# Inverting the diagonal blocks of all RWKV heads in one 128-partition loop instead of two 64-partition loops

## The chip, the cores and the metric

One core of a Trainium2 chip runs the whole program. The metric is the device time of one execution in microseconds, taken as the median of several runs. The engines are TensorE (PE for its matrix products, PEld for loading the stationary operand), VectorE (DVE), ScalarE (ACT), GpSimd (POOL) and SyncE (SP, which here issues nearly all DMAs). Each engine works through its own queue strictly in order and waits on semaphores for the others.

## What is computed

Two layers of a hybrid block (a pooling mixer, a retention branch, an RWKV-7 branch, three gated merges), followed by one attention layer and a mixture of experts. There are 512 tokens of width 1024. The change touches the RWKV-7 branch of each of the two layers. Its recurrence per head is, in the reference:

```
def step(S, inp):
    r_t, w_t, k_t, v_t, a_t, b_t = inp
    sa = jnp.einsum('bhvk,bhk->bhv', S, a_t)
    S = (S * w_t[:, :, None, :] + sa[..., None] * b_t[:, :, None, :]
         + v_t[..., None] * k_t[:, :, None, :])
    return S, jnp.einsum('bhvk,bhk->bhv', S, r_t)
```

There are 8 heads of width 64. The kernel does not walk the 512 tokens one by one: it cuts them into 8 chunks of 64 and solves, for each head and chunk, a unit triangular system of size 64. For this it inverts the two diagonal blocks of 32 x 32 of each system by elimination and puts the inverse of the whole together with two small products.

## The kernel before

The 8 heads are worked in two halves of 4 heads (`hf` 0 and 1). For one half there are three pieces of work, each a Python generator:

- `rwkv_prep` (line 557) scales the operands with the decay (DVE, ACT, POOL and a few products on PE), computes the masked products of all chunks (lines 635 to 651, called Gram products below; they go to DRAM as `gd`), and then inverts the diagonal blocks. For this, `lt` gets the blocks from DRAM with one block on each partition: 32 systems (4 heads by 8 chunks) times 2 diagonal blocks, so 64 partitions (line 667). The elimination has 31 turns of two DVE instructions each, a product into `tmp` (line 674) and an addition into `tt` (line 676); turn j works on (j+1)(31-j) elements of each partition, between 31 and 256. Then ACT turns one block over (line 681), and three DMAs write the results back to DRAM (lines 682 and 684), where the recurrence reads them.
- `rwkv_chain` (line 688) is the recurrence over the 8 chunks: a chain of small products on PE, with copies on DVE and ACT between them. Its products are tied one to the next by hand, and the first product of the next dense tile is tied behind them (`self.pin`), so PE can't run past a product of the recurrence that waits.
- `rwkv_out` (line 842) normalises and adds.

These generators run as side work of the dense matmuls, which fill PE with three passes (high and low parts) over each weight tile. `mm3` (line 309) calls `tick`, and each `tick` advances the side work: a dense tile with 8 contraction blocks gives two steps of it, one with 4 blocks gives one. A `yield` ends a step. What is emitted in which step decides the program order; a planner then orders each engine's queue by its own estimate of when an instruction is ready, and program order ranks the ready ones.

In `rwkv` (line 503) the first half's prep comes first (19 steps). Then the recurrence of half 0, which idles `CHAIN_WAIT` = 24 steps before its first loads, goes in turn with the prep of half 1, which waits `PREP_WAIT` = 6 steps and until its projections exist. The recurrence of half 1 follows with the output of half 0. `layer` (line 1095) starts this side work right after the projections of half 0; the retention branch (`rows_of` at 952, the projections of half 1, then q and k tiles with `rotary` at 1017), the pooling branch and the two first merges run meanwhile, and `self.drain(rs)` (line 1122) runs what is left of it before the third merge.

The dense weights pass through `split` (line 298): ACT rounds the high part, DVE (every fifth time POOL) subtracts it to get the low part `wlo` (line 306). PE needs both before it can run the tile, so DVE and ACT feed PE at every tile.

Of the kernel before, what the change touches and what calls it, by code (L numbers as in the profile page):

```python
# [11 lines left out]
F32 = mybir.dt.float32  # L12
F32R = mybir.dt.float32r
I32 = mybir.dt.int32
AF = mybir.ActivationFunctionType
OP = mybir.AluOpType
# [8 lines left out]
NC_ = T // C  # L25
# [150 lines left out]
class Layers:  # L176
# [324 lines left out]
        return out  # L501

    def rwkv(self, l, t, wa, out):
        prep = lambda hf: self.rwkv_prep(l, hf, t[hf][0:2], t[hf][2:4], t[hf][4:6], wa)
        ops = yield from prep(0)
        ys, nxt = yield from self.both(self.rwkv_chain(l, *ops, wait=CHAIN_WAIT), self.late(t, prep))
        (_, ys) = yield from self.both(self.rwkv_out(0, ys, ops[3]), self.rwkv_chain(l, *nxt))
        yield from self.rwkv_out(1, ys, nxt[3])
        out += ops[3] + nxt[3]

    def late(self, t, prep):
        for _ in range(PREP_WAIT):
            yield
        while len(t) < 2:
            yield
        return (yield from prep(1))

    def both(self, *gens):

# [37 lines left out]
    def rwkv_prep(self, l, hf, r, k, v, wa):  # L557

        nc, c = self.nc, self.c
# [4 lines left out]
        for i in range(2):  # L564
            p = 2 * hf + i
# [10 lines left out]
        DC = self.S("DC", [128, 2, NC_], "DC", 2)  # L576
        AR, BK, bv = [], [], []
        for i in range(2):
            p = 2 * hf + i
# [48 lines left out]
            nc.vector.tensor_mul(bk[:, :, :C], b3(kk), b3(di))  # L628
            AR.append(ar)
            BK.append(bk)  # L630
            yield

        nu = 4 * NC_
        gd = self.dr.tile([128, nu, 128], F32, name=f"gd{l}{hf}")
        for ch in range(0, NC_, 2):
            g = [self.RM() for _ in range(2)]
            m = None
            for j in range(4):
                for h2 in range(2):
                    r2 = slice(64 * h2, 64 * h2 + 64)  # L640
                    m = self.mm(g[h2][:, j * 128:j * 128 + 128], BK[j % 2][r2, ch + j // 2, :],
                                AR[j % 2][r2, ch + j // 2, :], start=True, stop=True, after=m)
            for h2 in range(2):
# [11 lines left out]
        if hf == 0:  # L655
            ad = self.dr.tile([128, 2, NC_, 128], F32, name=f"ad{l}")
            for i in range(2):
                nc.sync.dma_start(ad[:, i], AR[i])
            AR = ad

        lt = self.S("lt", [2 * nu, 32, 32], "b", NB)
        tt = self.S("tt", [2 * nu, 32, 32], "b", NB)
        nc.gpsimd.memset(tt, 0.0)
        nc.gpsimd.memset(tt.rearrange("p a b -> p (a b)")[:, ::33], 1.0)
        blk = lambda f: gd[32 * f:32 * f + 32, :, 32 * f:32 * f + 32].rearrange("s u t -> u s t")
        for f in range(2):
            nc.sync.dma_start(lt[nu * f:nu * f + nu], blk(f))
        yield
        yield
        tmp = self.S("tmp", [2 * nu, 16 * 16], "tmp", 1)  # L670
        for j in range(31):
            n = 31 - j
            t = tmp[:, :(j + 1) * n].rearrange("p (s t) -> p s t", s=j + 1)
            nc.vector.tensor_tensor(t, tt[:, 0:j + 1, j:j + 1].to_broadcast([2 * nu, j + 1, n]),  # L674
                                    lt[:, j:j + 1, j + 1:].to_broadcast([2 * nu, j + 1, n]), op=OP.mult)
            nc.vector.tensor_add(tt[:, 0:j + 1, j + 1:], tt[:, 0:j + 1, j + 1:], t)  # L676
            if j % 8 == 7:
                yield
        tn = self.dr.tile([32, nu, 32], F32, name=f"tn{l}{hf}")
        tu = lt[0:nu]  # L680
        nc.scalar.activation(tu, tt[0:nu].rearrange("p s t -> p t s"), AF.Copy)
        nc.sync.dma_start(tn.rearrange("t u s -> u t s"), tu)
        for f in range(2):
            nc.sync.dma_start(blk(f), tt[nu * f:nu * f + nu])
        yield
        return AR, BK, v, bv, DC, gd, tn

    def rwkv_chain(self, l, AR, BT, v, bv, DC, gd, tn, wait=0):

        nc, c = self.nc, self.c  # L690
        ident = c["ident"]
        u_of = lambda hd: (hd % 2) * 2 + hd // 2
        gts, ars, tis, xxs, brs, uvs, qys, ys = {}, {}, {}, {}, {}, {}, {}, []
# [62 lines left out]
            nc.vector.tensor_copy(q, qys[ch][0:64, :256])  # L756
            return q

        for _ in range(wait):
            yield  # L760
        for ch in range(3):
            load(ch)
        load_ar(1)
# [12 lines left out]
        for ch in range(NC_):  # L776
# [15 lines left out]
            if not last:  # L792
                for i in range(2):
                    for h2 in range(2):
                        s = slice(64 * h2, 64 * h2 + 64)
# [11 lines left out]
            if not last:  # L807
                for h2 in range(2):
                    s = slice(64 * h2, 64 * h2 + 64)
# [9 lines left out]
            o = 256 * (ch % 4 // 2)  # L819
# [1113 lines left out]
NB = 8  # L1933
# [5 lines left out]
ATT_RATE = 4.0  # L1939
NEX = 5  # L1940
NOH = 3
CHAIN_WAIT = 24
PREP_WAIT = 6


# [14 lines left out]
```

## Time and profile before

| | |
|---|---|
| median of 3 runs | 1994.51 us (1987.49 to 1998.53) |
| the profiled execution | 1992.5 us, its span from first to last instruction 1990.4 us |
| granted TensorE clock, mean | 0.959 of full speed |
| busy share of the span | PE 93%, DVE 55%, ACT 30%, POOL 26% |

The profile is of one execution. "Busy" of an engine is the time in which one of its instructions ran. The granted clock is given as a share of full speed: 1.0 is 2.4 GHz, 0.5 is 1.2 GHz, and a value between is a mean over a stretch with both. A matmul at half clock is busy for longer and does no more, so a stretch loses time for PE in two ways: it stands idle, or it runs at the low clock.

### The profile page before, as it was taken

How to read it: one execution, taken by the hardware profiler on the slowest of the kernel's cores; microseconds unless marked ns; L12 is line 12 of the kernel's file. 1: busy time of each engine (PE TensorE's matmuls, PEld its weight loads, DVE VectorE, ACT ScalarE, POOL GpSimd, SP SyncE). 2: the span in 40 equal slices, each digit the busy share in tenths (PEclk: the TensorE clock that was granted, in tenths of full speed). 3: DMA queues.
4: the chain of work that ended last, by engine and by line, in shares of the span. 5: the costliest groups of instructions: out<-in, count | busy, mean ns of one | idle time of the engine just before them, and what ended most of it. 6: DMA issues, size and time to landing. Idle time of an engine off the chain costs nothing. (4 is left out here: it accounts for less than half of the span.)

```text
span 1990.4 us, 26507 instructions
## 1 busy us (share of the span) xinstructions
PE 1854.2 (93%) x10194; PEld 1364.6 (69%) x10194; DVE 1095.2 (55%) x2333; ACT 588.7 (30%) x1054; POOL 520.5 (26%) x399
## 2 busy tenths in 40 slices
PE   6899698999999989988899999999999998999996
PEld 3767476777777867766677778787778777444443
DVE  4645979644543555498764443356564545343335
ACT  3332222333222333222233332253343334111112
POOL 1342553355565201234310122220110122100000
PEclk9989889999999989997899999999999979899998
DMA  7424242434443533423232323244322324899981
GB/s 301 138 72 120 70 140 62 126 129 124 125 136 99 165 94 95 118 67 89 75 90 89 92 75 106 79 124 157 113 80 66 112 101 191 354 424 419 402 343 43
DMA packets 103128, 288.90 MB, mean 145 GB/s; under 512 B 31112, under 2 KB 44296, under 8 KB 94808
## 3 DMA queue, kind: packets, MB, share of 16 engines
q1 hardware_dynamic: 97912, 267.27, 39.7%
q0 software_dynamic: 5088, 19.93, 2.7%
q8 instruction: 81, 1.33, 0.3%
q14 instruction: 47, 0.39, 0.1%
HBM read 268.77 MB, written 21.01 MB: 146 GB/s over the span
## 5 line engine op out<-in xcount | busy, mean ns | idle before, releaser
L350 PE MATMUL mm<-lo,whi 128*128 128x512 f32 x1424 | 568.0, 399 | 2.3 <-DVE lo L327 2.2
L350 PE MATMUL mm<-hi,wlo 128*128 128x512 f32 x1424 | 566.8, 399 | 2.3 <-DVE wlo L306 2.0
L350 PE MATMUL mm<-hi,whi 128*128 128x512 f32 x1320 | 530.3, 402 | 24.8 <-DVE ry L1023 7.9
L303 ACT ACTIVATE whi<-wst 128x1024 fp32r<-128x1024 f32 (+1 forms) x202 | 192.9, 956 | 567.2 <-PE mm L350 409.7
L350 PEld LDWEIGHTS mm<-hi,wlo 128*128 128x128 f32 x1424 | 272.1, 191 | 68.6 <-issue 4.8
L350 PEld LDWEIGHTS mm<-hi,whi 128*128 128x128 f32 x1320 | 252.5, 192 | 94.5 <-issue 9.8
L350 PEld LDWEIGHTS mm<-lo,whi 128*128 128x128 f32 x1424 | 272.4, 191 | 64.2 <-issue 4.5
L306 DVE TENSOR_TENSOR wlo<-wst,whi 128x1024 fp32r<-128x1024 f32 (+1 forms) x162 | 193.6, 1196 | 168.7 <-ACT whi L303 166.3
L306 POOL TENSOR_TENSOR wlo<-wst,whi 128x1024 fp32r<-128x1024 f32 (+1 forms) x40 | 90.8, 2269 | 329.3 <-ACT whi L303 255.9
L1798 PE MATMUL pp<-eg,xt 128*64 128x512 f32 x512 | 114.1, 598 | 0.2 <-PEq L1848 0.2
L433 POOL TENSOR_TENSOR wad<-wad,cact 128x1024 f32<-128x1024 f32 x32 | 63.1, 1973 | 167.2 <-DMA wad<-wada 152.5
L435 POOL TENSOR_TENSOR wad<-wad 128x512 f32<-128x512 f32 (+2 forms) x96 | 93.9, 978 | 6.0
L1798 PEld LDWEIGHTS pp<-eg,xt 128*64 128x64 f32 x512 | 37.0, 138 | 74.2 <-issue 73.8
L350 PE MATMUL mm<-vhi,hi 128*128 128x256 f32 x256 | 76.5, 302 | 7.0 <-ACT vhi L966 4.4
L904 POOL TENSOR_TENSOR acc<-acc,tg 128x512 f32<-128x512 f32 x32 | 50.0, 1564 | 108.0 <-DVE tg L902 97.5
L350 PE MATMUL mm<-vlo,hi 128*128 128x256 f32 x256 | 76.2, 299 | 0.7 <-DVE vlo L967 0.6
L350 PE MATMUL mm<-vhi,lo 128*128 128x256 f32 x256 | 75.3, 295 | 0.0
L1838 PE MATMUL mm<-y,ohT 128*128 128x512 f32 x256 | 69.2, 409 | 3.2 <-DVE xr L1840 1.6
L1766 POOL DMA_INDIRECT xg<-hx,idx x16 | 15.5, 969 | 204.7 <-DVE xt L1789 150.5
L674 DVE TENSOR_TENSOR tmp<-tt,lt 64x31 f32<-64x31 f32 (+15 forms) x124 | 57.7, 465 | 9.4 <-DMA lt<-gd 7.6
L676 DVE TENSOR_TENSOR tt<-tt,tmp 64x31 f32<-64x31 f32 (+15 forms) x124 | 61.7, 498 | 1.5
L1823 PE MATMUL ms<-ed,eht 128*64 128x512 f32 x256 | 58.7, 599 | 4.2 <-ACT eht L1813 4.0
(407 smaller groups left out, 2818.7 us busy)
## 6 DMA issues: line engine op xcount, KB each, us to landing
wst<-win SPq DMA_DIRECT2D x154, 512.0 KB, 3.7
eg<-egu SPq DMA_DIRECT2D x31, 2048.0 KB, 14.8
ed<-edn SPq DMA_DIRECT2D x31, 1024.0 KB, 10.8
wad<-wada SPq DMA_DIRECT2D x48, 512.0 KB, 4.5
wst<-wbr SPq DMA_DIRECT2D x48, 256.0 KB, 2.9
gd<-gs SPq DMA_DIRECT2D x64, 128.0 KB, 1.9
gt<-gd SPq DMA_DIRECT2D x32, 256.0 KB, 3.2
wst<-wout SPq DMA_DIRECT2D x16, 512.0 KB, 3.8
```

The costliest lines, as they stand in the source:

```text
L303: nc.scalar.activation(hi, w, AF.Copy)
L306: e.tensor_tensor(lo, w, hi.bitcast(F32), op=OP.subtract)
L350: return op(*args, **kw)
L433: nc.gpsimd.tensor_tensor(w, w, self.cact.unsqueeze(2).to_broadcast([128, 8, 128]), op=OP.mult)
L435: nc.gpsimd.tensor_add(w[:, :n], w[:, :n], w[:, n:2 * n])
L674: nc.vector.tensor_tensor(t, tt[:, 0:j + 1, j:j + 1].to_broadcast([2 * nu, j + 1, n]), lt[:, j:j + 1, j + 1:].to_broadcast([2 * nu, j + 1, ...
L676: nc.vector.tensor_add(tt[:, 0:j + 1, j + 1:], tt[:, 0:j + 1, j + 1:], t)
L904: nc.gpsimd.tensor_add(acc[d], acc[d], t)
L1766: self.last_row = self.nc.gpsimd.indirect_dma_start(xg, None, self.hx[:, :], bass.IndirectOffsetOnAxis(ap=idx, axis=0))
L1798: nc.tensor.matmul(p[64 * i:64 * i + 64], x[:, k, 64 * i:64 * i + 64], wts[e + i][0][:, k], start=k == 0, stop=k == 7)
L1823: nc.tensor.matmul(py[64 * i:64 * i + 64], ht[:, 128 * k + 64 * i:128 * k + 64 * i + 64], wts[e + i][1][:, k, 512 * c:512 * c + 512], star ...
L1838: nc.tensor.matmul(p, oT[:, 128 * tb:128 * tb + 128], y, start=i == 0, stop=i == len(parts) - 1)
```

## The change

The inversion leaves `rwkv_prep` and becomes a generator of its own, `inverses`, which takes both halves at once. `lt` and `tt` get 128 partitions, ordered so that the first diagonal blocks of both halves lie on the lower 64 and the second ones on the upper 64. The loop has the same 31 turns with the same elements on each partition, and runs once for each layer where it ran twice. ACT turns 64 partitions over at once; the DMAs keep their sizes and number. `rwkv` now prepares half 0, then half 1, then inverts, idles `CHAIN_WAIT` = 14 steps, and runs the recurrence of half 0; the rest is as before. `PREP_WAIT` goes.

```diff
     def rwkv(self, l, t, wa, out):
-        prep = lambda hf: self.rwkv_prep(l, hf, t[hf][0:2], t[hf][2:4], t[hf][4:6], wa)
-        ops = yield from prep(0)
-        ys, nxt = yield from self.both(self.rwkv_chain(l, *ops, wait=CHAIN_WAIT), self.late(t, prep))
-        (_, ys) = yield from self.both(self.rwkv_out(0, ys, ops[3]), self.rwkv_chain(l, *nxt))
-        yield from self.rwkv_out(1, ys, nxt[3])
+        ops = []
+        for hf in range(2):
+            while len(t) <= hf:
+                yield
+            ops.append((yield from self.rwkv_prep(l, hf, t[hf][0:2], t[hf][2:4], t[hf][4:6], wa)))
+        tn = yield from self.inverses(l, [o[5] for o in ops])
+        for _ in range(CHAIN_WAIT):
+            yield
+        ys = yield from self.rwkv_chain(l, *ops[0], tn[0])
+        (_, ys) = yield from self.both(self.rwkv_out(0, ys, ops[0][3]), self.rwkv_chain(l, *ops[1], tn[1]))
+        yield from self.rwkv_out(1, ys, ops[1][3])
...
-        lt = self.S("lt", [2 * nu, 32, 32], "b", NB)
-        tt = self.S("tt", [2 * nu, 32, 32], "b", NB)
+        return AR, BK, v, bv, DC, gd
+
+    def inverses(self, l, gds):
+        nu = 4 * NC_
+        lt = self.S("lt", [4 * nu, 32, 32], "b", NB)
+        tt = self.S("tt", [4 * nu, 32, 32], "b", NB)
...
-        for f in range(2):
-            nc.sync.dma_start(lt[nu * f:nu * f + nu], blk(f))
+        part = lambda t, hf, f: t[(2 * f + hf) * nu:(2 * f + hf + 1) * nu]
+        for hf in range(2):
+            for f in range(2):
+                nc.sync.dma_start(part(lt, hf, f), blk(hf, f))
         yield
         yield
...
-            nc.vector.tensor_tensor(t, tt[:, 0:j + 1, j:j + 1].to_broadcast([2 * nu, j + 1, n]),
-                                    lt[:, j:j + 1, j + 1:].to_broadcast([2 * nu, j + 1, n]), op=OP.mult)
+            nc.vector.tensor_tensor(t, tt[:, 0:j + 1, j:j + 1].to_broadcast([4 * nu, j + 1, n]),
+                                    lt[:, j:j + 1, j + 1:].to_broadcast([4 * nu, j + 1, n]), op=OP.mult)
             nc.vector.tensor_add(tt[:, 0:j + 1, j + 1:], tt[:, 0:j + 1, j + 1:], t)
             if j % 8 == 7:
                 yield
...
-        nc.scalar.activation(tu, tt[0:nu].rearrange("p s t -> p t s"), AF.Copy)
+        nc.scalar.activation(tu, tt[0:2 * nu].rearrange("p s t -> p t s"), AF.Copy)
...
-CHAIN_WAIT = 24
-PREP_WAIT = 6
+CHAIN_WAIT = 14
```

## Rows read from the trace of the kernel before

**Rows 1.** The page, part 1: busy time, share of the span, instructions.

```profile
PE 1854.2 (93%) x10194; PEld 1364.6 (69%) x10194; DVE 1095.2 (55%) x2333; ACT 588.7 (30%) x1054; POOL 520.5 (26%) x399
```

**Rows 2.** Stretches: length, then busy us (instructions) of each engine, granted clock, DMA.

```profile
core 0: us, PE busy (x) PEld busy (x) DVE busy (x) ACT busy (x) POOL busy (x), PEclk, DMA share, GB/s
100.00:150.00 50.00, 46.72 (x226) 34.22 (x224) 24.85 (x39) 14.96 (x29) 24.85 (x21) 0.86 0.22 74
183.00:258.00 75.00, 57.69 (x233) 39.62 (x234) 73.04 (x142) 16.56 (x23) 36.76 (x19) 0.87 0.20 64
292.00:347.00 55.00, 47.76 (x317) 37.47 (x316) 51.38 (x126) 15.38 (x26) 24.82 (x19) 0.94 0.24 68
755.00:815.00 60.00, 57.67 (x325) 45.92 (x324) 34.26 (x58) 18.80 (x36) 10.51 (x9) 0.97 0.25 82
850.00:904.00 54.00, 43.92 (x191) 32.56 (x190) 52.96 (x109) 11.10 (x14) 20.49 (x11) 0.94 0.22 61
904.00:930.00 26.00, 23.29 (x81) 16.45 (x82) 21.60 (x36) 7.85 (x10) 10.54 (x9) 0.67 0.33 91
960.00:1005.00 45.00, 39.05 (x262) 31.31 (x261) 40.30 (x114) 11.37 (x22) 11.21 (x9) 0.90 0.18 51
1040.00:1250.00 210.00, 210.00 (x1405) 165.13 (x1404) 88.23 (x205) 65.42 (x113) 43.02 (x27) 1.00 0.31 91
```

**Rows 3.** The same view for tile `tt` alone: DVE, ACT, POOL busy, clock, DMA.

```profile
183.00:258.00 75.00, 33.26 (x62) 0.45 (x1) 0.00 (x0) 0.87 0.20 64
```

**Rows 4.** Waits of PE from 183 to 258 us: total, times, longest.

```profile
PE rm L616 <- DVE rw L614: 10.1, 1, 10.1
PE rm L582 <- DVE rw L617: 1.5, 1, 1.5
```

**Rows 5.** Waits of PE from 850 to 930 us.

```profile
PE mm L350 <- DVE ry L1023: 5.8, 4, 2.7
PE rm L616 <- DVE rw L614: 2.7, 1, 2.7
PE rm L582 <- DVE rw L617: 0.9, 1, 0.9
```

**Rows 6.** The page, part 5: the loop's two lines in the whole span.

```profile
L674 DVE TENSOR_TENSOR tmp<-tt,lt 64x31 f32<-64x31 f32 (+15 forms) x124 | 57.7, 465 | 9.4 <-DMA lt<-gd 7.6
L676 DVE TENSOR_TENSOR tt<-tt,tmp 64x31 f32<-64x31 f32 (+15 forms) x124 | 61.7, 498 | 1.5
```

**Rows 7.** Groups by shape on DVE: busy us, mean ns of one.

```profile
L1022 DVE TENSOR_TENSOR ry<-mm,sin 64x512 f32<-64x512 f32 x16 | 11.1, 693 | 0.2
L1020 DVE TENSOR_TENSOR rx<-mm,cos 128x512 f32<-128x512 f32 x16 | 10.8, 678 | 0.1
```

**Rows 8.** Instructions in order of time, on POOL and then on DVE: start, length.

```profile
216.44 5.15 POOL L306 TENSOR_TENSOR wlo<-wst,whi 128x1024 fp32r<-128x1024 f32 x1
...
219.29 2.58 DVE L676 TENSOR_TENSOR tt<-tt,tmp 64x255 f32<-64x255 f32 x1
...
223.26 0.42 DVE L676 TENSOR_TENSOR tt<-tt,tmp 64x255 f32<-64x255 f32 x1
...
961.59 0.18 DVE L674 TENSOR_TENSOR tmp<-tt,lt 64x31 f32<-64x31 f32 x1 [0.91 <-DMA lt<-gd]
```

**Rows 9.** Waits of SP's queue from 300 to 360 us.

```profile
SPq L684 <- DVE tt L676: 12.3, 1, 12.3
```

**Rows 10.** Line 681 (ACT) in layer 0, and the landings of line 667.

```profile
L681 ACT ACTIVATE lt<-tt x2: 1975/2020/2066, 257.6 to 345.6; 32x1024 f32<-32x1024 f32 x2
...
DMA to landing us min/median/max: 2.3/2.8/3.8
```

**Rows 11.** DVE in order of time: loop ends, and the third chunk's copy in half 0.

```profile
292.75 0.51 DVE L674 TENSOR_TENSOR tmp<-tt,lt 64x31 f32<-64x31 f32 x1 [0.72 <-DMA lt<-gd]
...
345.36 0.20 DVE L676 TENSOR_TENSOR tt<-tt,tmp 64x31 f32<-64x31 f32 x1
...
360.97 0.41 DVE L787 COPY uv<-rm 64x256 f32<-64x256 f32 x1
...
1021.89 0.42 DVE L787 COPY uv<-rm 64x256 f32<-64x256 f32 x1 [0.75 <-PE rm L352]
```

More of the change, by code (lines that the diff above doesn't have):

```diff
@@ L503, in rwkv @@
     def rwkv(self, l, t, wa, out):
-        prep = lambda hf: self.rwkv_prep(l, hf, t[hf][0:2], t[hf][2:4], t[hf][4:6], wa)
-        ops = yield from prep(0)
-        ys, nxt = yield from self.both(self.rwkv_chain(l, *ops, wait=CHAIN_WAIT), self.late(t, prep))
-        (_, ys) = yield from self.both(self.rwkv_out(0, ys, ops[3]), self.rwkv_chain(l, *nxt))
-        yield from self.rwkv_out(1, ys, nxt[3])
-        out += ops[3] + nxt[3]
-    def late(self, t, prep):
-        for _ in range(PREP_WAIT):
+        ops = []
[5 more added lines that the diff above has]
+        for _ in range(CHAIN_WAIT):
             yield
-        while len(t) < 2:
-            yield
-        return (yield from prep(1))
+        ys = yield from self.rwkv_chain(l, *ops[0], tn[0])
+        (_, ys) = yield from self.both(self.rwkv_out(0, ys, ops[0][3]), self.rwkv_chain(l, *ops[1], tn[1]))
+        yield from self.rwkv_out(1, ys, ops[1][3])
+        out += ops[0][3] + ops[1][3]
     def both(self, *gens):
@@ L659, in rwkv_prep @@
             AR = ad
-        lt = self.S("lt", [2 * nu, 32, 32], "b", NB)
-        tt = self.S("tt", [2 * nu, 32, 32], "b", NB)
+        return AR, BK, v, bv, DC, gd
+    def inverses(self, l, gds):
+        nc = self.nc
+        nu = 4 * NC_
+        lt = self.S("lt", [4 * nu, 32, 32], "b", NB)
+        tt = self.S("tt", [4 * nu, 32, 32], "b", NB)
         nc.gpsimd.memset(tt, 0.0)
         nc.gpsimd.memset(tt.rearrange("p a b -> p (a b)")[:, ::33], 1.0)
-        blk = lambda f: gd[32 * f:32 * f + 32, :, 32 * f:32 * f + 32].rearrange("s u t -> u s t")
-        for f in range(2):
-            nc.sync.dma_start(lt[nu * f:nu * f + nu], blk(f))
+        blk = lambda hf, f: gds[hf][32 * f:32 * f + 32, :, 32 * f:32 * f + 32].rearrange("s u t -> u s t")
+        part = lambda t, hf, f: t[(2 * f + hf) * nu:(2 * f + hf + 1) * nu]
+        for hf in range(2):
+            for f in range(2):
+                nc.sync.dma_start(part(lt, hf, f), blk(hf, f))
         yield
         yield
-        tmp = self.S("tmp", [2 * nu, 16 * 16], "tmp", 1)
+        tmp = self.S("tmp", [4 * nu, 16 * 16], "tmp", 1)
         for j in range(31):
@@ L678, in rwkv_prep, with rwkv_chain @@
                 yield
-        tn = self.dr.tile([32, nu, 32], F32, name=f"tn{l}{hf}")
-        tu = lt[0:nu]
-        nc.scalar.activation(tu, tt[0:nu].rearrange("p s t -> p t s"), AF.Copy)
-        nc.sync.dma_start(tn.rearrange("t u s -> u t s"), tu)
-        for f in range(2):
-            nc.sync.dma_start(blk(f), tt[nu * f:nu * f + nu])
+        tu = lt[0:2 * nu]
+        nc.scalar.activation(tu, tt[0:2 * nu].rearrange("p s t -> p t s"), AF.Copy)
+        tns = []
+        for hf in range(2):
+            tn = self.dr.tile([32, nu, 32], F32, name=f"tn{l}{hf}")
+            tns.append(tn)
+            nc.sync.dma_start(tn.rearrange("t u s -> u t s"), part(lt, hf, 0))
+            for f in range(2):
+                nc.sync.dma_start(blk(hf, f), part(tt, hf, f))
         yield
-        return AR, BK, v, bv, DC, gd, tn
-    def rwkv_chain(self, l, AR, BT, v, bv, DC, gd, tn, wait=0):
+        return tns
+    def rwkv_chain(self, l, AR, BT, v, bv, DC, gd, tn):
         nc, c = self.nc, self.c
@@ L757, in right @@
             return q
-        for _ in range(wait):
-            yield
         for ch in range(3):
```

## The prediction

> **What bounds the kernel now.** I read the page's busy shares first: PE is busy for 93% of the span and DVE for 55% [rows 1]. That looks like a kernel in which DVE work is free. The share is a mean over stages, so I then cut the two RWKV layers into stretches [rows 2] and asked in each for two things: how long PE stood idle, and how far its granted clock was below 1.0. I price a stretch as idle time plus (1 - clock) x length. That is a little too much, since part of a low clock falls into idle time.
>
> The loop runs four times, and wherever it runs DVE is full. Layer 0: half 0 from 183 to 258 us (DVE 73.04 of 75), half 1 from 292 to 347 us (51.38 of 55). Layer 1: half 0 from 850 us on (52.96 of 54 to 904), half 1 from 960 to 1005 us (40.30 of 45). PE loses there [rows 2]:
>
> - A, 183 to 258: 17.3 idle + 0.13 x 75 = 9.8, together 27.1 us
> - B, 292 to 347: 7.2 + 3.3 = 10.5 us
> - C, 850 to 930: 10.1 + 3.2 in its first stretch, 2.7 + 8.6 in its second (clock 0.67), together 24.6 us
> - D, 960 to 1005: 6.0 + 4.5 = 10.5 us
>
> That is 73 us. Against it, from 1040 to 1250 us, where both recurrences run and no loop does, PE is busy for 210.00 of 210 us at clock 1.00 [rows 2]: the recurrences by themselves cost PE no waiting.
>
> Who is waited for in A and C? In A PE waits 10.1 us for line 614 and 1.5 us for line 617, in C 5.8 us for the rotary products (line 1023) and 2.7 us for line 614 [rows 4, 5]. None of these is the loop. They are the prep of half 1 and the retention branch, late because they stand in DVE's queue between the loop's instructions: of DVE's 73 us in A the loop has 33.3 [rows 2, 3]. So the loop of half 0 collides with the prep of half 1, and PE pays.
>
> **Part by part: the halved loop.** The loop's two lines hold 57.7 + 61.7 = 119.4 us in 248 instructions, about 30 us for each of the four runs [rows 6]. The trace has no 128-partition form of it, but it has neighbours: 64 x 512 products take 693 ns, 128 x 512 ones 678 ns [rows 7]. Length goes by the elements on a partition, not by the partitions. So 124 DVE instructions and 60 us of DVE go, 30 us in each layer. ACT turns the same 1024 elements on a partition, 2.0 us [rows 10], twice less often. None of this is on PE.
>
> **The half-0 loop leaves A and C.** DVE keeps 73 - 33 = 40 us of work in A, while PE has 75 - 27 = 48 us of it at full clock. DVE then has slack, but what is left is still a prep, a chain across DVE, ACT, POOL and PE. What a prep without a loop costs can be read: half 0's own, at 100 to 150 us in layer 0, loses 3.3 + 7.0 = 10.3 us, and at 755 to 815 us in layer 1 loses 2.3 + 1.8 = 4.1 us [rows 2]. I leave these prices standing: A gives 27.1 - 10.3 = 16.8 us, C gives 24.6 - 4.1 = 20.5 us.
>
> **The joint loop in B and D.** It takes the place of half 1's loop with the same DVE time, but without the recurrence of half 0 beside it, which now starts later. Bounds: nothing is won (0) or all of it (21.0). I take the middle, 10.5 us, for the pooling and retention work beside it stays.
>
> **The moved recurrences.** A step is one advance of the side work. Before: the first recurrence loads at step 19 + 24 = 43, the last output ends at 43 + 27 + 27 + 4 = 101. After: half 0's prep ends at 13, half 1's starts when its projections exist (step 20, for 8 ticks of the v rows and 6 tiles of 2 have run) and ends at 33, the inversion takes 6 (39), the idling 14 (53), and the end is 53 + 27 + 27 + 4 = 111. From the start of the side work to the drain at line 1122 there are 8 + 12 + 16 + 16 + 24 + 8 + 24 + 8 + 8 = 124 steps. So 13 are left, and no remainder is drained without cover. Moving a recurrence into the first merges costs nothing [rows 2], as its row from 1040 us shows.
>
> **The added wait.** The first recurrence now stands 14 steps behind the loop instead of 24 behind its own half's. Its first product needs the loop's result, and the next dense tile is tied behind that product, so a late loop stops PE. The recurrence's loads move 10 steps later, to where the third chunk's copy stood: 360.97 in layer 0, 1021.89 in layer 1. The joint loop replaces the one that began at 292.75 and 961.59 [rows 8, 11]. Everything moves earlier alike as A and C shrink, so the distances hold: 68 and 60 us, less some 5 us for what B and D shrink: 63 and 55. The loop took 345.4 - 292.8 = 53 us in B and 43 us in D (961.6 to the stretch's end) [rows 2, 8, 11], then come 2.0 us on ACT and two landings of some 2.8 us [rows 10], 7.6 us. Slack: 2 and 4 us. Too little to be sure: between 0 and 8 us of stop in a layer I take 4, so -8 us in all.
>
> **Queues moved past.** SP's queue stands at line 684 until the loop ends, up to 12.3 us [rows 9], with weight loads behind it; this now happens once in a layer with six DMAs, not twice with three. The four loads of `lt` go one after the other ahead of the loop, so its first instruction may hold DVE's queue for one more landing, 2.8 us [rows 10]; both within the 4 us above. POOL clears `tt` once, off any path. The eight big buffers are full when `lt` and `tt` want theirs; two are free by then, since half 0's `ar` has gone to DRAM.
>
> **Sum.** 16.8 + 20.5 + 10.5 - 8 = 39.8 us. The profiled execution had 1990.4 + 2.1 = 1992.5 us, so 1952.7 for it; that run lay 2.0 us under the median, so 1955 for the median.
>
> **A rule weighed against the trace.** A product of 255 elements took 2.58 us in A and 0.42 us four microseconds later; the long one ended at 221.87 us, where a POOL subtraction of 5.15 us (it began at 216.44) ended at 221.59 [rows 8]. A part of the loop's 30 us is therefore waiting for POOL. From 0.42 us at 255 elements and 0.18 us at 31 I estimate an undisturbed loop: 1.07 ns for each element, 0.147 us for each instruction, 62 x 0.147 + 10912 x 1.07 ns = 21 us.
> The Trainium skill (SBUF — State Buffer, "Who interferes with whom") says that a VectorE instruction with two SBUF inputs and a GpSimd instruction that reads SBUF exclude each other for a whole instruction. By that rule 9 of the 30 us belong to POOL's work, and the next DVE instruction with two inputs would inherit them; the sum by it is the rival "small relief". The pair of rows agrees with it.
>
> **Rivals.**
> *Small relief.* POOL has the same work in A, so its share of the waiting stays, and only 21 of 30 us go. A and C then give 0.7 x 37.3 = 26 us, B and D nothing, the late start costs 8: 18 us, 1976. If the planner, which orders by its own estimates, gives back only the waits that the rows name as late prep (10.1 + 1.5 + 2.7 + 0.9 = 15.2) [rows 4, 5], less 8, it is 7 us: 1987. For it: POOL is busy 36.8 of 75 us in A [rows 2]. Against: DVE keeps slack even so.
>
> *The recurrence waits for the loop: slower.* In A a loop beside a prep and the rotary products took all of 75 us [rows 3]. If the joint loop is stretched so, it ends 75 - 53 = 22 us and 75 - 43 = 32 us later than I count, less the slack of 2 and 4, and PE stands behind the pinned product: 48 us instead of 8. After such gaps the clock was 0.67 for 26 us [rows 2], 8.6 us more in each layer. 1955 + 40 + 17 = 2012. It decides from a loop of about 55 us in layer 0 and 48 us in layer 1. For it: rotary work of the later heads still runs at the loop's new place. Against: it met a full prep in A, which is now done before.
>
> *It does not halve.* If 128 partitions took twice as long, the loop's DVE time would stay, all of it in B and D; A and C win 37, B and D lose about as much: 1995. [Rows 7] speak against it.
>
> **How the numbers follow.** Forecast (1932 to 1977) 0.62; small relief at its lower end (near 1987) 0.18; recurrence waits 0.14; does not halve 0.03; still more, as all of B and D comes back and no start is late, 0.03 (1994.5 - 37.3 - 21 = 1936 and below). The range takes in the forecast and the small relief: 1932 to 1990. About 0.5%, 10 us, is what a measurement here tells from no change. Faster (below 1984.5): 0.62 + 0.03 + 0.05 of the small relief = 0.70. Same: 0.13 + 0.03 + 0.01 = 0.17. Slower: 0.13.
>
> **What would show it.** Lines 674 and 676 with 62 instructions each of about the same mean, 60 us in all. In the prep of half 1 (the stretch after line 572's second run in a layer) DVE below 85%, and PE's wait for line 614 down from 10.1 to under 3 us. In the loop's stretch DVE still above 85%, and PE losing around 5 us. Between the loop's end and the first product of the recurrence a PE wait of under 5 us. I'm wrong if that wait is tens of us, if PE waits as long in the prep as before with DVE idle (the chain, not the queue, was the limit), or if the loop's mean doubles.

## The result and the profile after

The changed kernel takes 1969.99 us (median; 1965.73 to 1971.92), the kernel before measured beside it 1996.52 us. The ratio is 0.9873, with a 95% interval of 0.9836 to 0.9909. The change makes the kernel 26 us faster. Forecast were 1955 us, a range of 1932 to 1990, and 39.8 us of gain. The profiled execution has a span of 1966.7 us (before 1990.4).

Busy time, share of the span and instructions (the page, part 1):

```profile
PE 1846.0 (94%) x10194; PEld 1361.0 (69%) x10194; DVE 1051.8 (53%) x2209; ACT 584.8 (30%) x1052; POOL 506.2 (26%) x395
```

124 DVE instructions are gone. Against [rows 1], DVE is 43.4 us less busy and PE 8.2 us less, with the same number of products. That is less than the loop lost: its two lines fell from 119.4 us [rows 6] to 57.1, so the other 2085 DVE instructions took 18.9 us longer than before. The loop's two lines, now 680 and 682 (count, then shortest, median and longest duration in ns, first and last start):

```profile
L680 DVE TENSOR_TENSOR tmp<-tt,lt x62: 178/382/1306, 277.5 to 956.3; 128x31 f32<-128x31 f32 x4, 128x60 f32<-128x60 f32 x4, 128x87 f32<-128x87 f32 x4, 128x112 f32<-128x112 f32 x4
L682 DVE TENSOR_TENSOR tt<-tt,tmp x62: 184/391/2554, 277.7 to 957.1; 128x31 f32<-128x31 f32 x4, 128x60 f32<-128x60 f32 x4, 128x87 f32<-128x87 f32 x4, 128x112 f32<-128x112 f32 x4
```

The loop runs from 277.5 to 325.8 us in layer 0 and from 916.5 to 957.3 us in layer 1. The stretches that answer to [rows 2], in this order: half 0's prep, half 1's prep, the loop and what follows it in layer 0, half 1's prep and the loop in layer 1, both recurrences:

```profile
core 0: us, PE busy (x) PEld busy (x) DVE busy (x) ACT busy (x) POOL busy (x), PEclk, DMA share, GB/s
100.00:150.00 50.00, 46.71 (x253) 35.39 (x253) 26.31 (x40) 15.29 (x29) 24.73 (x19) 0.97 0.28 90
180.00:245.00 65.00, 57.08 (x246) 41.06 (x245) 55.52 (x83) 16.53 (x22) 33.09 (x23) 0.92 0.26 73
277.00:328.00 51.00, 40.57 (x163) 32.26 (x163) 45.35 (x107) 9.04 (x12) 18.57 (x16) 0.83 0.21 58
328.00:365.00 37.00, 31.30 (x178) 22.59 (x177) 19.29 (x40) 11.16 (x22) 9.84 (x7) 0.82 0.41 107
845.00:912.00 67.00, 66.07 (x336) 49.04 (x335) 56.27 (x88) 16.88 (x24) 34.86 (x23) 0.97 0.35 98
912.00:960.00 48.00, 36.03 (x148) 27.71 (x148) 43.54 (x115) 11.95 (x15) 15.21 (x12) 0.86 0.25 63
1040.00:1230.00 190.00, 190.00 (x1337) 149.10 (x1336) 85.61 (x203) 59.81 (x105) 42.59 (x27) 1.00 0.30 89
```

and tile `tt` alone in the two stretches of the loop (DVE, ACT, POOL busy):

```profile
277.00:328.00 51.00, 30.74 (x62) 2.07 (x1) 0.00 (x0) 0.83 0.21 58
912.00:960.00 48.00, 26.37 (x62) 2.05 (x1) 0.00 (x0) 0.86 0.25 63
```

Two stretches of before have no row in the front of this document: the ones behind B and behind C.

```profile
347.00:380.00 33.00, 28.66 (x213) 21.97 (x212) 21.53 (x49) 13.18 (x24) 9.02 (x7) 1.00 0.38 104
930.00:960.00 30.00, 28.18 (x189) 21.61 (x187) 19.28 (x40) 7.39 (x13) 13.24 (x10) 0.93 0.45 131
```

Priced as the prediction does it, idle time plus (1 - clock) x length:

| | before | after | gain |
|---|---|---|---|
| A, prep of half 1 in layer 0 | 27.1 | 7.9 + 5.2 = 13.1 | 14.0 |
| C, the same in layer 1 (with 930 to 960) | 24.6 + 3.9 | 0.9 + 2.0 = 2.9 | 25.6 |
| B, loop in layer 0 | 10.5 | 10.4 + 8.7 = 19.1 | -8.6 |
| D, loop in layer 1 | 10.5 | 12.0 + 6.7 = 18.7 | -8.2 |
| behind the loop of layer 0 | 4.3 | 5.7 + 6.7 = 12.4 | -8.1 |
| 100 to 150, prep of half 0 | 10.3 | 3.3 + 1.5 = 4.8 | 5.5 |

Together this is 20.2 us of the span's 23.7. By layers it is -2.7 us in layer 0 (A, B and the stretch behind the loop) and 17.4 us in layer 1 (C and D). Two of the sizes seem to belong to one execution and not to the change. One is the last line: in the experiment that leaves out half 1's loop, where this prep is the same code in the same place, the same 50 us had PE busy for 46.70 at a clock of 1.00. The other is the clock of 0.82 behind the loop of layer 0, 6.7 us. In three runs below (5 to 7), in which the loop keeps its place, that stretch ran at 1.00 and lost 4.0 to 4.3 us, as before the change (rows of runs 5 and 7):

```profile
328.00:365.00 37.00, 32.66 (x215) 24.65 (x214) 20.68 (x49) 14.35 (x24) 11.61 (x9) 1.00 0.45 113
328.00:365.00 37.00, 32.97 (x218) 24.84 (x217) 19.82 (x43) 13.74 (x27) 11.21 (x8) 1.00 0.46 121
```

So the preps gave what was forecast, and nearly half of it went again in the stretches where the joint loop runs. There PE waits for DVE (waits of PE, total, times, longest; first in layer 0 from 272 to 330 us, then in layer 1 from 912 to 962 us):

```profile
PE mm L350 <- DVE th L887: 4.9, 1, 4.9
PE ms L1097 <- DVE sm L879: 3.1, 1, 3.1
PE ms L954 <- POOL wad L435: 2.0, 1, 2.0
PE mm L350 <- ACT u L929: 1.8, 1, 1.8
...
PE ms L954 <- DVE ws L950: 7.2, 1, 7.2
PE mm L350 <- DVE th L887: 4.0, 1, 4.0
```

Line 887 is the SiLU of the pooling branch's gates, line 950 makes the pooling branch's tiles, and line 879 is the retention branch's normalisation. As in A before, PE doesn't wait for the loop, but for mixers' tiles whose place in DVE's queue is between the loop's instructions. The wait for the SiLU isn't new: before (its line was 880), PE waited for it in B and in D too.

```profile
PE mm L352 <- DVE th L880: 3.2, 1, 3.2
...
PE mm L352 <- DVE th L880: 4.7, 1, 4.7
```

### The profile page after: what moved, and what is told of

Same layout as the page of the kernel before. It is cut to its first block, busy times and chain, and to the rows that moved or that the text cites. A ratio compares the mean times of both kernels' runs of the same rounds, so it can differ in the third digit from the quotient of the medians.

```text
span 1966.7 us, 26375 instructions
## 1 busy us (share of the span) xinstructions
PE 1846.0 (94%) x10194; PEld 1361.0 (69%) x10194; DVE 1051.8 (53%) x2209; ACT 584.8 (30%) x1052; POOL 506.2 (26%) x395
## 5 line engine op out<-in xcount | busy, mean ns | idle before, releaser
L1773 POOL DMA_INDIRECT xg<-hx,idx x16 | 15.5, 969 | 205.5 <-DVE xt L1796 151.3
L1845 PEld LDWEIGHTS mm<-y,ohT 128*128 128x128 f32 x256 | 44.8, 188 | 23.3 <-DVE xr L1847 13.0
L350 PEld LDWEIGHTS mm<-vhi,hi 128*128 128x128 f32 x256 | 50.6, 199 | 14.4 <-issue 6.2
```

Of the source, the lines that this page charges most:

```text
L350: return op(*args, **kw)
L1773: self.last_row = self.nc.gpsimd.indirect_dma_start(xg, None, self.hx[:, :], bass.IndirectOffsetOnAxis(ap=idx, axis=0))
L1845: nc.tensor.matmul(p, oT[:, 128 * tb:128 * tb + 128], y, start=i == 0, stop=i == len(parts) - 1)
```

## Experiments

Each time stands as a ratio to the kernel before, run beside it on the same chip. A thousandth is 2 us.

**1 and 2. What does each half's loop cost in the kernel before?** In one run half 0's loop is replaced by one addition, which leaves the elimination out, in the other half 1's:

```diff
+        if hf == 0:        # second run: hf == 1
+            nc.vector.tensor_add(tt, tt, lt)
+            for _ in range(3):
+                yield
+        else:
...
```

> Leaves out: the kernel before, with the 31 turns of half 0's loop replaced by one addition (identity plus the block), so the inverse of half 0 is only its first order; all else stays. DVE loses about 60 us (62 instructions in each layer). My step 'the half-0 loop leaves A and C' gives 16.8 + 20.5 = 37 us for exactly this, so 1958 to 1962 where before is 1996. Theory 'only the waits named in the rows come back': 15 us, about 1981. Theory 'DVE time is hidden anyway': within 5 us of before.

> Leaves out: the kernel before, with half 1's loop replaced by one addition. My pricing of stretches B and D (21 us lost there) says at most 21 us, about 1975 to 1985, if the loop is what costs PE there. Rival: half 1's loop lies beside the recurrence, which gives PE other work and little DVE work, so it costs less than half 0's: under 10 us, 1987 or more.

Measured: without half 0's loop 0.9883 [0.9851, 0.9915], without half 1's 0.9882 [0.9852, 0.9913]: 23 us each. For half 1's loop that is about what B and D lose (21.0); in its windows, B and D lose 3.9 and 0.0 us, so 17.1 us come back there:

```profile
292.00:347.00 55.00, 54.41 (x329) 42.38 (x330) 30.82 (x81) 17.26 (x31) 22.33 (x20) 0.94 0.31 86
960.00:1005.00 45.00, 45.00 (x312) 35.16 (x312) 26.88 (x70) 16.82 (x30) 9.24 (x8) 1.00 0.22 66
```

The rival that this loop costs under 10 us, because the recurrence beside it keeps PE at work, is out. For half 0's loop the 23 us are less than the 37.3 us which the prediction took out of A and C. The windows of the first of these runs show why (A, then the three stretches that follow it):

```profile
180.00:255.00 75.00, 69.77 (x330) 52.43 (x330) 66.64 (x100) 22.30 (x28) 36.12 (x26) 0.98 0.34 99
255.00:290.00 35.00, 26.26 (x174) 20.52 (x173) 21.68 (x36) 6.38 (x12) 19.66 (x15) 0.81 0.44 129
290.00:337.00 47.00, 44.87 (x281) 35.62 (x281) 45.85 (x114) 9.88 (x17) 16.88 (x15) 0.96 0.20 60
337.00:375.00 38.00, 29.82 (x194) 23.15 (x194) 22.78 (x52) 14.57 (x25) 9.05 (x7) 0.91 0.37 102
```

A falls from 27.1 us lost to 5.2 + 1.5 = 6.7. But right behind it, where before lost about 1 us (258 to 292 us: PE busy 33.65 of 34), 8.7 + 6.7 = 15.4 are lost, and 8.2 + 3.4 = 11.6 from 337 us on instead of 4.3. DVE's share doesn't explain these: DVE is busy for only 21.68 of 35 us in the first. There PE waits for line 877's retention tile (4.0) and line 646's masked product (3.2), in the second for line 927's activation (6.0). It looks as if a relieved stretch brings PE sooner to chains that aren't done; that a part of its gain is lost behind it is what the windows show.

**3. What does the joint loop still cost?** The changed kernel with one addition in place of the loop.

> Leaves out: the changed kernel with the joint loop replaced by one addition. What is left of the joint loop's cost: the trace of the changed kernel shows about 19 us of lost PE time in each of the two stretches with the loop, and 12 us at the first product of the recurrence in layer 0 against 4 before. Theory 'DVE queue full': all of these but some 5 us each come back, 25 to 35 us, 1935 to 1945. Rival 'the pooling and retention work is late by itself there' (a chain between DVE, POOL and PE): under 12 us, 1958 or more.

Measured: 1934.7 us, 0.9712 [0.9677, 0.9747]. The joint loop costs 0.9873 - 0.9712 = 0.0161, 32 us. Both of before cost 23 + 23 if they add up. The loop's own stretch then loses 2.7 + 1.5 = 4.2 us instead of 19.1, and the one behind it 1.1 instead of 12.4:

```profile
279.00:330.00 51.00, 48.35 (x268) 37.87 (x267) 30.00 (x72) 16.14 (x24) 22.86 (x19) 0.97 0.37 100
330.00:365.00 35.00, 33.89 (x218) 26.64 (x217) 16.35 (x29) 11.52 (x20) 13.62 (x10) 1.00 0.44 137
```

So the loss in the loop's stretch is the loop's doing. So is what is lost behind it, apart from the 6.7 us of clock there, which runs 5 to 7 don't have with the loop in place.

**4. Order or halving?** The changed order with two loops of 64 partitions one after the other:

```diff
-        for j in range(31):
+        for q in (slice(0, 2 * nu), slice(2 * nu, 4 * nu)):
+            for j in range(31):
...
+                nc.vector.tensor_add(tt[q, 0:j + 1, j + 1:], tt[q, 0:j + 1, j + 1:], t)
```

> Nothing left out: the changed order (both halves prepared, then the inversion), but the inversion as two loops on 64 partitions, one after the other, in the place of the joint one. DVE keeps its 248 loop instructions. Theory 'the halving is the gain' (the loop is moved, and 30 us of DVE in each layer go): the second loop adds 30 us of DVE to stretches where DVE is full, and the recurrence waits for it: 2005 or more, slower than both kernels. Rival 'the order is the gain' (the loop no longer collides with the prep): within 10 us of the changed kernel, 1965 to 1980.

Measured: 2014.87 us, 1.0114 [1.0082, 1.0146]. The new order alone, in which the recurrence of half 0 also has to wait for both loops, is 23 us slower than before, and the halving is worth 1.0114 - 0.9873 = 0.0241, 48 us. Windows of the two loop stretches:

```profile
274.00:348.00 74.00, 46.94 (x166) 35.67 (x164) 70.03 (x169) 8.31 (x12) 20.53 (x17) 0.73 0.12 36
940.00:1012.00 72.00, 44.14 (x177) 34.70 (x175) 66.09 (x178) 11.51 (x16) 13.91 (x12) 0.79 0.17 47
```

PE is idle for 27 and 28 us and runs at mean clocks of 0.73 and 0.79. For the recurrence's first product it waits 6.1 us in layer 0 and not at all in layer 1. In this order the first loop's worth of DVE time costs 32 us, the second 48. The second one comes on top of a DVE that the first has filled; how much of the 48 us that makes, no run tells apart from the recurrence's later start.

**5 to 7. Do steps place the loop or the recurrence?** Three runs change only when the side work is emitted: `CHAIN_WAIT` 20; a `yield` after every 2 turns and `CHAIN_WAIT` 2; 16 idle steps ahead of the inversion and `CHAIN_WAIT` 8.

```diff
+        for _ in range(INV_WAIT):        # third run: 16
+            yield
         tn = yield from self.inverses(l, [o[5] for o in ops])
```

> The changed kernel with 20 idle steps between the inversion and the recurrence instead of 14; nothing left out. In the changed kernel PE waits 3.6 us for the inverse's landing in layer 0, and the stretch 328 to 365 us around it loses 12 us against 1 without a loop. Theory 'the recurrence stands too close behind the loop': that wait goes, 6 to 10 us faster than the changed kernel, 1960 to 1964. Rival 'the loss there is the loop's own, its low clock and late pooling tiles': within 4 us of it, 1966 to 1974.

> The changed kernel, the loop emitted two turns to a step over 15 steps instead of eight turns to a step over 3, and 2 idle steps behind it instead of 14, so the recurrence starts at the same step. Theory 'rank': the loop's 62 instructions are emitted early and so go ahead of what the dense and pooling tiles need from DVE; paced, these go first, and the 19 and 17 us lost in the loop's two stretches fall to some 8 each: 15 to 20 us faster than the changed kernel, 1950 to 1955. Theory 'load': 30 us more of DVE work in a stretch that is already full cost the same in any order, within 5 us of it, 1965 to 1975. A third outcome: the recurrence waits longer for the loop, slower.

> The changed kernel with the whole inversion 16 steps later (behind the pooling tiles, in the first merge) and 8 idle steps behind it instead of 14; the recurrences end at step 122 of 124. Theory 'load': in the first merge DVE is about 40% busy, so the loop finds room and its two stretches lose some 10 us less each: 1945 to 1955. Theory 'rank': no better, since the loop's instructions go ahead of the low parts of the weights there: 1965 to 1975. Risk told beforehand: the end of the recurrence meets the drain, up to 10 us slower.

Measured: 0.9893 [0.9863, 0.9922], 0.9873 [0.9835, 0.9911], 0.9865 [0.9834, 0.9895]: all as the changed kernel. The expectations on the loop's place and order (runs 6 and 7) were not put to the test, since the loop did not move. With 16 more idle steps its first instruction began at

```profile
276.82 1.25 DVE L682 TENSOR_TENSOR tmp<-tt,lt 128x31 f32<-128x31 f32 x1 [0.20 <-DMA lt<-gd]
```

where it began at 277.51 without them. In the three runs it began at 276.8 to 282.2 us in layer 0 and at 911.1 to 919.4 in layer 1 (changed kernel: 277.5 and 916.5). The planner seems to take the loop as soon as its data can be there; what is counted in steps says nothing here about when it runs. The recurrence did move in part: its first copy (line 794) stayed within 4 us in layer 0, but its last one came 19 to 24 us later in runs 5 and 7, at no measurable price. For run 5 that favours its rival, that the loss behind the loop isn't a matter of the distance: PE's wait for the inverse fell only from 3.6 to 2.5 us.

**8 and 9. The same two questions, with the loop held.** Now instructions of the loop may be issued only behind the low part (line 306) that DVE was given last. In run 8 this holds every pair of turns, with a `yield` after each and `CHAIN_WAIT` 2: meant to be spread in the same place. In run 9 it holds the first turn alone, with 16 idle steps ahead and `CHAIN_WAIT` 8: later, not spread.

```diff
+        i = e.tensor_tensor(lo, w, hi.bitcast(F32), op=OP.subtract)
+        if e is nc.vector:
+            self.low = i
...
+            with self.tc.issue_after(self.low.ins):        # run 9: for j == 0 only
                 nc.vector.tensor_tensor(t, ...)
                 nc.vector.tensor_add(...)
```

> The changed kernel, with the joint loop spread in DVE's queue: each pair of turns may be issued only behind the low part that was emitted last, the loop yields after every 2 turns (it yielded after 8), and CHAIN_WAIT is 2, so that the recurrence isn't later by this. Two theories for the 35 us that the joint loop still costs. Load: DVE is near full in that stretch, and 30 us more of it cost PE the same in whatever order they are queued; then about as the changed kernel, 1965 to 1975. Order: what costs is that loop instructions run back to back while a low part or a pooling tile stands behind them; spread out, at most four loop instructions (about 2 us) stand ahead of any of these, PE's waits on DVE in the stretch (4.9, 3.1 and 2.0 us in layer 0) go to under 1 us each, and the time falls to 1950 to 1955. Should the loop be spread so far that the recurrence waits for it, PE waits at the recurrence's first products and the time is above 1980.

> The changed kernel, with the inversion 16 steps later, this time held there: its first turn is issued behind the low part emitted at that step, and CHAIN_WAIT is 8. In the run with 16 idle steps alone the loop began where it did before. The loop then begins some 25 to 40 us later, in the first merge, where DVE has less work of the mixers. If the price of the loop is that it falls into a stretch in which DVE is near full (pooling and rotary products), DVE's slack there takes it: 1940 to 1955, with less than 5 us lost in the loop's own stretch in layer 0 (it was 18.4). If the loop costs the same wherever it runs, 1965 to 1975. If the recurrence then ends behind the side work's last step and is run without cover, or PE waits for the loop at the first product, above 1980.

Measured: run 8 0.9864 [0.9820, 0.9908], no different from the changed kernel. But it tells little: in layer 0 its DVE queue has 23, 9, 9 and 21 instructions of the loop from one low part to the next, as the changed kernel's has. The low part behind which they were held was long past, and the three longest waits of PE are the same to a tenth (4.9, 3.1, 2.0). In layer 1 only the last 10 of the 62 instructions were spread.

The late run takes 1950.33 us, 0.9801 [0.9760, 0.9842]. In it the loop runs from 299.7 to 345.8 and from 942.2 to 983.5 us (windows of the loop in layer 0, what follows it, and the loop in layer 1):

```profile
299.00:348.00 49.00, 38.41 (x162) 30.02 (x162) 44.18 (x108) 12.66 (x20) 18.07 (x13) 0.90 0.19 62
348.00:385.00 37.00, 35.56 (x206) 28.48 (x206) 10.54 (x15) 10.96 (x19) 13.58 (x10) 1.00 0.65 177
942.00:984.00 42.00, 38.43 (x171) 30.28 (x170) 38.79 (x106) 12.47 (x21) 6.58 (x5) 0.96 0.20 59
```

Lost are 15.5, 1.4 and 5.3 us, where the changed kernel loses 19.1, 12.4 and 18.7. In layer 0 that misses the expectation of under 5 us: DVE is 90% busy there even so, and of the 11.0 us behind the loop 6.7 are the clock of one execution. The largest part is layer 1's loop, 13.4 us. The three stretches together lose 28.0 us less and the kernel 14, so here too a part is lost elsewhere: from 245 to 299 us run 9 loses 5.0 us, the changed kernel 1.8 from 245 to 277. The loop isn't spread (31, 12, 17 and 2 of its instructions from one low part to the next), so it is the later place that won 14 us: the loop's, and with it the recurrence's, whose first copy came at 381.6 us instead of 350.4.

**10 to 12. How late, and spread as well?** Run 10: as run 9 with 24 idle steps and `CHAIN_WAIT` 2. Runs 11 and 12: late and spread, every pair of turns held, with 16 and with 8 idle steps.

> As the run with 16 idle steps and the first turn of the loop held behind the low part emitted there (1950), but with 24 steps, and CHAIN_WAIT 2. In that run the loop began 22 us later in layer 0 and 29 us later in layer 1 than in the changed kernel, and the stretches around it lost 35.7 us instead of 52.1. If the gain came from the loop leaving the mixers' stretch, which the retention and pooling branch fill, another 8 steps (about 15 us) take it further out: 1940 to 1950. If it came from there already having been reached, the same: 1947 to 1955. The recurrence's first copy was at 382 us in layer 0, 36 us after the loop's end; it would now come at about 397, and the whole recurrence has 1 step left before the drain: if it runs over, PE waits in the drain ahead of the third merge (a new loss near 530 to 560 us), and the time is above 1955.

> The two held forms together: 16 idle steps ahead of the inversion, every pair of turns held behind the low part emitted last, CHAIN_WAIT 2. Spreading alone gave 1961 (0.9864 of the kernel before, where the changed kernel had 0.9873), so if order within the stretch costs nothing, this is as the late form alone, 1945 to 1955. If in the first merge, where DVE has fewer other tiles, the low parts are what wait behind the loop (PE waited there 5.3 us for line 929's activation, that is line 934 of that run, and 10.6 us were idle in all), spreading it takes 3 to 8 us off: 1940 to 1947. If the loop is stretched so that the recurrence's product waits for it, above 1955.

> Every pair of turns held behind the low part emitted last, as in the run with 16 idle steps ahead of the inversion, but with 8 idle steps; CHAIN_WAIT 2. With 16 steps the stretches around the loop lost least of all runs with a whole loop (27.8 us from 200 to 400, 5.6 us from 900 to 1050), but the last copy of the recurrence's second half came 14 and 23 us later than without spreading (588 and 1225 us against 574 and 1202), and the two stretches about the third merge lost some 10 us more (waits for line 500's and 862's work and for ACT's split). If both of these are the causes, 8 steps give back the late end (last copies by 575 and 1205 us) and keep most of the gain in the loop's stretch: 1942 to 1950. If the gain in the loop's stretch came from the place alone, and not from the spreading, the loop falls back into the mixers' stretch: 1955 to 1965.

Measured: 24 steps 1992.4 us, 0.9991 [0.9973, 1.0009]. The whole gain is gone, most of it earlier than at the drain that was expected. In layer 0 PE waits only 3.6 us for the recurrence's first product, but 16.0 us for `wad` (POOL, line 437), side work whose loads came late: by the profile, SP's loads (line 293) waited 26.2 us for DVE's loop instructions from 340 to 400 us. In layer 1 the loop ends at 1034.7 us, and PE stands for the first product. PE in order of time, one line of each layer:

```profile
387.15 0.59 PE L441 MATMUL ms<-ones,wad 128*128 128x1 f32 x2 [11.53 <-POOL wad L437]
...
1043.98 0.31 PE L352 MATMUL rm<-ti,gt 32*32 32x32 f32 x2 [16.80 <-DMA ti<-tn]
```

In layer 1 this is the rival "the recurrence waits for the loop" in a kernel that brings it about. From 1260 to 1300 us, behind the recurrence's end, 8.9 us more are lost. Late and spread by 16 steps: 0.9831 [0.9803, 0.9859]; the loop's stretches lose only 10.4 and 2.7 us, but the recurrence's last copy comes at 588 and 1225 us instead of run 9's 574 and 1202. About the third merge, from 420 to 660 us, 14.4 us are lost instead of run 9's 3.6. For the first product PE doesn't wait; that outcome above 1955 us has another reason than the one expected. With 8 steps: 1952.37 us, 0.9800 [0.9779, 0.9821], between the two ranges of the expectation, so it decides for neither; the last copies come at 565 and 1197 us. Windows of the loop in that run:

```profile
277.00:348.00 71.00, 60.15 (x258) 46.68 (x257) 63.52 (x142) 17.40 (x27) 28.73 (x23) 0.93 0.22 64
912.00:982.00 70.00, 61.31 (x288) 49.13 (x287) 55.85 (x141) 20.37 (x31) 18.88 (x14) 0.98 0.20 57
```

The loop starts where the changed kernel's does and takes 70 us instead of 48 and 41, with 2 to 16 of its instructions from one low part to the next in layer 0. Here order and place change together; no run changes the order alone. Runs 9 and 12 are both 14 us faster than the changed kernel and 40 us faster than before. That is the gain that the forecast had counted on, by an edit that the change itself doesn't contain.

## Why the prediction was right, and where it was not

The direction and the range held, and the rows that told of it were the right ones: DVE full in four stretches, not its 55% over the span. Point by point:

- **The halved loop: right.** 62 instructions on each line with 57.1 us in all ([rows 6]: 119.4); forecast 60. A turn on 128 partitions costs what it cost on 64. Run 4 shows that without this the change is slower than before. But DVE as a whole is only 43.4 us less busy, since its other instructions took 18.9 us longer; why, no run shows. (The two instructions of 255 elements in [rows 8] are additions, line 676, and not products as the prediction has it. Its comparison isn't touched by that.)
- **A and C: right in size, in the changed kernel's trace.** 14.0 and 21.7 us in the stretches counted, forecast 16.8 and 20.5. The wait for line 614 (now 613) is gone in layer 0 and 0.3 us in layer 1 ([rows 4, 5]: 10.1 and 2.7), where this is left:

```profile
PE rm L615 <- DVE rw L613: 0.3, 1, 0.3
```

  Of the 7.9 us that PE still idles in A, 6.7 are one wait for the retention branch's line 879. DVE is 85 and 84% busy in these preps, just at the 85% that was to be the sign. But run 1 shows that such a sum is no price: what is taken out of a stretch is partly lost behind it.
- **The joint loop in B and D: the step that failed.** Taken was a gain of 10.5 us, the middle of 0 and 21.0; measured is a loss of 16.8, outside these bounds. A loss of about 5 us in the loop's stretch was the sign; it is 19.1 and 18.7. The prediction left the loop "the same DVE time" and took the recurrence of half 0 away from beside it as relief. Run 3 shows that the loop makes this loss (without it 4.2 us instead of 19.1 in layer 0), and run 9 that the price hangs on where the loop stands, with run 10 for its limit. Why it is dearer here than half 1's loop was in B and D is argued and not shown. In B, PE had 317 instructions in 55 us [rows 2], in the changed kernel's loop 163 in 51. The recurrence's small products seem to have filled PE's gaps, while the dense work advanced at DVE's pace with them or without: from the first SiLU of the pooling branch to the third it took 34.1 us in B (300.99 to 335.13) and 38.4 us beside the joint loop (281.96 to 320.36). Run 2 limits this reading: half 1's loop had the recurrence beside it and cost 23 us all the same, and the 9 us from there to the joint loop's 32 are within the intervals. No run puts a recurrence beside the joint loop.
- **The added wait: right in size by luck, wrong in its working.** Forecast 8 us in all, 4 in a layer; measured are 8.1 in layer 0 and, from 960 to 1000 us, 0.7 lost in layer 1. The first product waited 3.6 us for `ti` in layer 0:

```profile
PE rm L350 <- DMA ti<-tn: 3.6, 1, 3.6
```

  Another 6.7 us of that stretch are the clock of one execution, and runs 5 to 7 lose there what the kernel before lost. So the late start cost little, and the 8 us were too much. The working counted steps between the loop and the recurrence. Runs 5 to 7 show that steps did not place the loop and moved the recurrence's start by a few us only in layer 0; the slack of 2 and 4 us was worth nothing as a number.
- **Queues moved past: right.** Ahead of the loop DVE's queue waited for `lt`, 0.58 us in layer 0 and 3.18 us in layer 1, where 2.8 had been named:

```profile
916.54 0.19 DVE L680 TENSOR_TENSOR tmp<-tt,lt 128x31 f32<-128x31 f32 x1 [3.18 <-issue]
```

  (The view names no releaser. Two loads of `lt` went out at 912.7 and 913.1 us there and landed 2.3 us later.) In the stretches of preps and loops PE waited for no weight load, and for a DMA only in the 3.6 us above.

Of the rivals, "does not halve" falls with the loop's rows and run 4. "The recurrence waits" did not happen with loops of 48 and 41 us, under the 55 and 48 from which it was to decide; run 10 shows its mechanism in layer 1 (16.8 us of wait), though its loss of some 40 us against run 9 has other parts too. "Small relief" gave 1976, nearer to the result than the forecast. One part of it fits: DVE as a whole gave back 43.4 of the loop's 62.3 us, the share of 21 in 30 that this rival had put. Its sum does not: A and C gave more than its 26 us, and B and D did not stay even.

Summed up in prices: the preps bring 35.7 us, the failed term takes 16.8 where 10.5 were to come, the stretch behind the loop takes 8.1, and the stretches that the sum didn't look at (930 to 960, the clock in half 0's prep) bring 9.4. That is the table's 20.2. Without the two clocks that belong to one execution (5.5 for and 6.7 against the change) it would be 21.4. The failed term is 27.3 us from what was taken, and the table stays 19.6 us short of the forecast's 39.8. The range held by its width.

## What to carry to other kernels

Work on an engine that is free on average has the price of the stretch in which it runs: leave it out once and look, before its relief is summed from stretches, and look at the stretch behind too. When work is joined or moved, read what will stand beside it at the new place: small products that keep PE busy without the other engine may be cover and not load (argued here from counts, not shown). Where a planner orders the queues, check where a moved instruction began before any count of program steps is believed; here only a hold behind a given instruction moved the loop (and not every hold did), and that was worth 14 us.

## What the runs showed of the hardware

The loop's DVE time went with what POOL did beside it. Its 62 instructions took 30.74 us with POOL busy for 18.57 us, and 26.37 with 15.21 (the rows of the changed kernel above). In layer 1 of run 10, POOL was all but idle (first all tiles, then `tt` alone):

```profile
1002.00:1035.00 33.00, 25.18 (x112) 20.51 (x110) 29.43 (x73) 7.46 (x11) 1.30 (x1) 0.96 0.32 96
1002.00:1035.00 33.00, 22.12 (x62) 0.30 (x1) 0.00 (x0) 0.96 0.32 96
```

22.12 us, where 21 us had been estimated for an undisturbed loop from two rows [rows 8]. In layer 0 of the same run it took 33.26 us with POOL busy for 17.56. No run changes POOL's work alone. The Trainium skill (SBUF — State Buffer, "Who interferes with whom") says that a VectorE instruction with two inputs in SBUF contends with a GpSimd instruction that reads SBUF; these rows agree. If all of the difference is such waiting, it is 8.6 of the loop's 30.74 us in layer 0 of the changed kernel; what it cost the kernel no run shows.

The price of a loop on DVE wasn't proportional to its time either: 30.7 and 26.4 us of it cost the kernel 32 us, and 101.7 us in run 4 cost 0.0402, 80 us, both against the kernel without it. The 80 us include what the recurrence's later start cost.
